# Final sums of a conditioning vector: columns through VectorE and small products, gates through two float32r products

## The chip, the cores and the metric

The kernel runs on one core of a Trainium2 chip. The metric is the device time of one execution in microseconds (us). TensorE (PE, with its weight loads as PEld), VectorE (DVE), ScalarE (ACT) and GpSimd (POOL) each work through their own instructions in the order in which the program placed them; SyncE (SP) issues nearly all loads of weights.

## The reference

Two decoder layers over 256 tokens of width 2048, all float32. Each layer has a mixer and a SwiGLU feed-forward block, and each block is wrapped alike:

```
def ada_modulation(c, w, b):
    mod = jax.nn.silu(c) @ w + b
    return jnp.split(mod[:, None, :], 6, axis=-1)
...
    sh_m, sc_m, gt_m, sh_f, sc_f, gt_f = ada_modulation(c, aw, ab)
    h = rmsnorm(x, m_pre) * (1.0 + sc_m) + sh_m
    x = x + gt_m * rmsnorm(mixer(h), m_post)
    h = rmsnorm(x, f_pre) * (1.0 + sc_f) + sh_f
    x = x + gt_f * rmsnorm(swiglu(h, wg, wu, wd), f_post)
```

The change concerns `ada_modulation` alone: for each layer a vector of 6 x 2048 numbers (the *sections*: shift, scale and gate for the mixer, and again for the feed-forward block) is the product of one vector with a 2048 x 12288 matrix. That matrix is 100 MB per layer, a third of all bytes that the kernel reads.

## The kernel before

**The large products.** Every weight is loaded in float32 as a tile `w` of 128 x 1024 (512 KB, a ring of 6), and split: ACT casts it to float32r (`wh`, L159), DVE subtracts to get the rest (`wl`, L160). Both go into rings of 3. `mm3` (L234 to L236) makes three float32r products of the two halves with the two halves of the activations. Nearly all of PE's time is in these three lines.

**The conditioning.** The generators `ada`, `ada_scale`, `ada_shift` and `ada_gate` are a background stream: `tick`, called from the loops over the large products, lets the stream take a step at a set rate (`AR`), so that the 100 MB of each layer are loaded between the weights, through the same ring of 6 `w` tiles. The first two sections of layer 0 are computed in `start` and are not touched by the change. Ten sections go through the stream, in the order gm0, hf0, sf0, gf0, hm1, sm1, gm1, hf1, sf1, gf1 (g is a gate, h a shift, s a scale; m the mixer, f the feed-forward block; the digit is the layer).

A section is made in two halves of 1024 columns. A tile `acc` of 128 x 1024 is zeroed by POOL (L340), its first row receives the bias by a small DMA (L341), and for 16 tiles of the matrix DVE adds weight times silu(c) to it (L355, 128 x 1024 each). For the section gm0 PE does that instead (L329), and DVE adds its partial sums (L349). There is one buffer for `acc`: the next half's zeroing waits until the last reader of this one is done.

What remains is to sum `acc` over its 128 partitions. Each half is cut into two pieces of 512 columns (`finish`, called with q = 0 to 3), so a half brings a *pair* of calls:

- shifts and scales need the sums as columns, 128 x 4. `to_cols` makes them with four products of a 128 x 128 piece of `acc` as the stationary operand and a single column of ones (L365). DVE then copies the four columns out (L374 or L385). 6 sections x 4 calls = 24 calls.
- gates need the sums in every partition. One product with a stationary 128 x 128 of ones and `acc` as the moving operand of 512 columns does it (L400), and DVE multiplies by the norm's weights (L402). 4 sections x 4 calls = 16 calls. For gm0 the column of ones is replaced by `sel`, which picks 4 of the 128 partitions.

All these products are in float32; the trace shows each as two instructions of PE.

**What sets the order.** The program is written once; a scheduler places the instructions on each engine by its own estimate of when each will be ready. Only the splits have a raised priority. An engine then runs its list strictly in that order: a DVE instruction that has to wait holds up every DVE instruction behind it, the splits among them.

Of the kernel before, what the change touches and what calls it, by code (L numbers as in the profile page):

```python
# [43 lines left out]
class Net:  # L44
# [49 lines left out]
    def consts(s):  # L94
        nc = s.nc

        def mask(name, op, cm, step, base=0):
            t = s.cst.tile([P, P], F32, name=name)
            nc.gpsimd.memset(t, 1.0)
            nc.gpsimd.affine_select(out=t, in_=t, pattern=[[step, P]], compare_op=op, fill=0.0, base=base, channel_multiplier=cm)  # L100
            return t

        s.ident = mask("ident", ALU.is_equal, 1, -1)
        s.uinc = mask("uinc", ALU.is_ge, -1, 1)
        s.ustr = mask("ustr", ALU.is_gt, -1, 1)
        s.lstr = mask("lstr", ALU.is_gt, 1, -1)
        s.ones = s.cst.tile([P, P], F32, name="ones")
        nc.gpsimd.memset(s.ones, 1.0)

        s.sel = s.cst.tile([P, LINE], F32, name="sel")[:, 0:1]  # L110
        nc.vector.tensor_reduce(out=s.sel, in_=s.ident[:, 0::32], axis=AX.X, op=ALU.add)

    def picks(s):
        nc = s.nc
# [216 lines left out]
    def ada(s, layer, sec, finish, pe=False):  # L331
# [5 lines left out]
        for hf in range(2):  # L337
# [18 lines left out]
                    if g < 15:  # L356
                        yield
            for q in range(2):
                finish(2 * hf + q, halves[q], s.sel if pe else s.ones)
            yield  # L360

    def to_cols(s, acc, e):
        ps = s.tp()
        for m in range(4):
            s.nc.tensor.matmul(ps[:, m : m + 1], lhsT=acc[:, m * P : m * P + P], rhs=e[:, 0:1], start=True, stop=True)  # L365
        return ps

    def ada_scale(s, layer, sec, pre, key, pe=False):
        t = s.cst.tile([P, 16], F32, name="S_" + key)

        def finish(q, acc, e):
            ps = s.to_cols(acc, e)
            qs = slice(4 * q, 4 * q + 4)
            s.nc.vector.scalar_tensor_tensor(out=t[:, qs], in0=ps[:, :4], scalar=1.0, in1=s.V[pre][:, qs], op0=ALU.add, op1=ALU.mult)  # L374
            if q == 3:
                s.mod[key] = t
# [3 lines left out]
    def ada_shift(s, layer, sec, key, pe=False):  # L380
        t = s.cst.tile([P, 16], F32, name="H_" + key)

        def finish(q, acc, e):
            ps = s.to_cols(acc, e)
            s.nc.vector.tensor_copy(t[:, 4 * q : 4 * q + 4], ps[:, :4])  # L385
            if q == 3:
                s.mod[key] = t
# [3 lines left out]
    def ada_gate(s, layer, sec, post, key, pe=False):  # L391
        g = []

        def finish(q, acc, e):
# [2 lines left out]
                g.append(s.b(name="gate"))  # L397
                s.pin(nc.gpsimd.dma_start(out=g[-1], in_=s.a[post][q * 512 : q * 512 + 1024].partition_broadcast(P)))
            ps = s.tp()
            nc.tensor.matmul(ps, lhsT=e[:, 0:1].to_broadcast([P, P]), rhs=acc, start=True, stop=True)  # L400
            gs = g[-1][:, (q % 2) * 512 : (q % 2) * 512 + 512]
            nc.vector.tensor_tensor(out=gs, in0=ps, in1=gs, op=ALU.mult)  # L402
            if q == 3:
# [1243 lines left out]
```

## Time and profile before

| | |
|---|---|
| three runs | 2548.6, 2556.36, 2563.09 us (median 2556.36) |
| the profiled execution | 2552.04 us, its span 2550.3 us |
| granted TensorE clock, mean | 0.978 |
| PE busy | 2433.1 us (95%) |
| DVE busy | 1722.2 us (68%) |
| ACT busy | 1106.1 us (43%) |
| column sums, L365 | 192 instructions of PE, 404 to 1652 us |
| gate sums, L400 | 32 instructions of PE, 242 to 2004 us |

A row of a group names the line, engine, operation, tiles, shapes and count, then the busy time in us and the mean duration of one in ns, then the idle time of the engine just before these instructions with what ended it. A row of the timeline begins with the start in us and the duration in us. Durations of PE instructions overlap, since it works pipelined: what an instruction costs there is the distance from one start to the next. A row of the windows has, after the stretch and its length, the busy time of each engine with its instructions, then the granted clock, the share of time in which the DMA engines were busy, and GB/s.

By time, the stages are: the start of layer 0 to about 320 us, its mixer to about 590 us, the first feed-forward block to 1370 us, the mixer of layer 1 to 1800 us, and the second feed-forward block. The calls in question lie at 242 and 317 us (gm0), 404 and 486 (hf0), 541 and 594 (sf0), 717 and 790 (gf0), 857 and 933 (hm1), 1009 and 1085 (sm1), 1158 and 1225 (gm1), 1304 and 1450 (hf1), 1556 and 1650 (sf1), 1739 and 2003 (gf1), each time a pair.

### The profile page before, as it was taken

The numbers are of one execution on the slowest core, as the hardware profiler recorded it, in microseconds if no ns is written. First come the engines' busy times: TensorE is split into PE (matmuls) and PEld (weight loads), VectorE is DVE, ScalarE is ACT, GpSimd is POOL, SyncE is SP. The second block draws the span as 40 slices with busy tenths as digits, with TensorE's granted clock in tenths as the row PEclk, the third lists the DMA queues.
The fourth block names the chain that finished last, engine by engine and source line by source line (L and its number), as shares of the span: only waits on it lengthen the run. The fifth ranks groups of instructions, "written<-read, shape, count | busy, mean of one in ns | idle before, by whom it ended". The sixth has DMA issues, their size and how long they took to land.

```text
span 2550.3 us, 43246 instructions
## 1 busy us (share of the span) xinstructions
PE 2433.1 (95%) x17510; PEld 2141.5 (84%) x17510; DVE 1722.2 (68%) x2268; ACT 1106.1 (43%) x1385; POOL 91.1 (4%) x153
## 2 busy tenths in 40 slices
PE   5999998997999999999998999999999999999998
PEld 2578877876899899989987897787799889988996
DVE  6856786878677766777778676677655544545456
ACT  3354552435344444433435533444544444443443
POOL 1120011000000000000000000000000000000000
PEclk8999998998999999999999999999999999999999
DMA  8877566686798888998886596788467666666664
GB/s 282 322 245 261 176 214 215 204 312 226 244 313 292 305 285 290 309 317 314 289 273 216 155 289 224 242 282 271 164 215 225 197 191 194 195 190 194 195 191 140
DMA packets 299017, 615.70 MB, mean 241 GB/s; under 512 B 24368, under 2 KB 61680, under 8 KB 298816
## 3 DMA queue, kind: packets, MB, share of 16 engines
q1 hardware_dynamic: 294240, 604.32, 71.5%
q0 software_dynamic: 2304, 4.93, 0.6%
q10 hardware_dynamic: 2272, 3.68, 0.4%
q8 instruction: 137, 2.24, 0.3%
q14 instruction: 64, 0.52, 0.1%
HBM read 610.10 MB, written 2.10 MB: 240 GB/s over the span
## 4 chain that ended last, share of the span: by engine, by line
PE 77%; DVE 8%; DMA 8%; ACT 3%; issue 3%; POOL 0%; ACTq 0%; DVEq 0%; SPq 0%
PE mm L236 23%; PE mm L235 23%; PE mm L234 23%; DMA w<-in_ada_w_dram 6%; DVE wl L160 2%; DVE small L355 1%; PE tp L329 1%; PE tp L365 1%; DMA w<-in_w_out_dram 1%; ACT small L462 1%; ACT small L421 1%; PE tp L1049 1%; ACT wh L159 0%; PE tp L400 0%; DMA w<-in_w_in_dram 0%
## 5 line engine op out<-in xcount | busy, mean ns | idle before, releaser
L159 ACT CAST wh<-w 128x1024 fp32r<-128x1024 f32 x722 | 758.0, 1051 | 1095.6 <-PE mm L235 550.6
L160 DVE TENSOR_TENSOR wl<-w,wh 128x1024 fp32r<-128x1024 f32 x722 | 874.1, 1220 | 476.0 <-ACT wh L159 474.9
L236 PE MATMUL mm<-hhi,wl 128*128 128x256 f32 (+1 forms) x3104 | 865.1, 279 | 10.0 <-DVE wl L160 10.0
L234 PE MATMUL mm<-hhi,wh 128*128 128x256 f32 (+1 forms) x3104 | 866.2, 279 | 0.0
L235 PE MATMUL mm<-hlo,wh 128*128 128x256 f32 (+1 forms) x3104 | 863.3, 278 | 0.0
L236 PEld LDWEIGHTS mm<-hhi,wl 128*128 128x128 f32 (+1 forms) x3104 | 582.8, 188 | 15.2 <-DVE wl L160 13.2
L235 PEld LDWEIGHTS mm<-hlo,wh 128*128 128x128 f32 (+1 forms) x3104 | 583.2, 188 | 2.0 <-issue 1.1
L234 PEld LDWEIGHTS mm<-hhi,wh 128*128 128x128 f32 (+1 forms) x3104 | 581.3, 187 | 4.1 <-issue 2.0
L355 DVE SCALAR_TENSOR_TENSOR small<-w,silu_c,small 128x1024 f32<-128x1024 f32 x288 | 369.0, 1281 | 195.8 <-DMA w<-in_ada_w_dram 187.3
L236 PE MATMUL mm<-wh,alo 128*128 128x512 f32 x656 | 258.2, 394 | 0.0
L235 PE MATMUL mm<-wl,ahi 128*128 128x512 f32 x656 | 256.9, 392 | 0.0
L234 PE MATMUL mm<-wh,ahi 128*128 128x512 f32 x656 | 256.2, 391 | 0.0
L234 PE MATMUL mm<-wh,hhi 128*128 128x512 f32 x440 | 177.1, 406 | 8.1 <-DVE hhi L467 4.2
L235 PE MATMUL mm<-wl,hhi 128*128 128x512 f32 x440 | 177.8, 404 | 3.5 <-DVE wl L160 2.2
L236 PE MATMUL mm<-wh,hlo 128*128 128x512 f32 x440 | 175.2, 399 | 0.7 <-DVE hlo L468 0.7
L235 PEld LDWEIGHTS mm<-wl,ahi 128*128 128x128 f32 x656 | 123.1, 188 | 29.1 <-issue 0.5
L234 PEld LDWEIGHTS mm<-wh,ahi 128*128 128x128 f32 x656 | 123.2, 188 | 27.2 <-ACT wh L159 0.5
L236 PEld LDWEIGHTS mm<-wh,alo 128*128 128x128 f32 x656 | 123.3, 188 | 25.1
L234 PEld LDWEIGHTS mm<-wh,hhi 128*128 128x128 f32 x440 | 83.8, 192 | 27.7 <-ACT wh L159 5.5
L236 PEld LDWEIGHTS mm<-wh,hlo 128*128 128x128 f32 x440 | 84.6, 192 | 22.3 <-issue 2.3
L235 PEld LDWEIGHTS mm<-wl,hhi 128*128 128x128 f32 x440 | 84.4, 192 | 22.4 <-DVE wl L160 3.9
L329 PE MATMUL tp<-w,silu_c 128*32 128x512 f32 x384 | 67.0, 645 | 11.6 <-DMA w<-in_ada_w_dram 6.7
(438 smaller groups left out, 2325.5 us busy)
## 6 DMA issues: line engine op xcount, KB each, us to landing
w<-in_ada_w_dram SPq DMA_DIRECT2D x384, 512.0 KB, 5.2
w<-in_ffn_gate_dram SPq DMA_DIRECT2D x176, 512.0 KB, 4.6
w<-in_ffn_up_dram SPq DMA_DIRECT2D x176, 512.0 KB, 4.5
w<-in_ffn_down_dram SPq DMA_DIRECT2D x176, 512.0 KB, 4.5
w<-in_w_in_dram SPq DMA_DIRECT2D x160, 512.0 KB, 5.2
w<-in_w_out_dram SPq DMA_DIRECT2D x64, 512.0 KB, 5.3
w<-in_s_glu_w_dram SPq DMA_DIRECT2D x8, 512.0 KB, 5.0
x<-in_x_dram SPq DMA_DIRECT2D x4, 512.0 KB, 6.4
```

The lines of the kernel that those rows point to most:

```text
L159: s.nc.scalar.copy(hi, x)
L160: s.subs.append(s.nc.vector.tensor_tensor(out=lo, in0=x, in1=hi, op=ALU.subtract).ins)
L234: mm(ps, lhsT=lhs[0], rhs=rhs[0], start=st, stop=False)
L235: mm(ps, lhsT=lhs[0], rhs=rhs[1], start=False, stop=False)
L236: mm(ps, lhsT=lhs[1], rhs=rhs[0], start=False, stop=en)
L329: s.nc.tensor.matmul(ps[32 * j : 32 * j + 32, :], lhsT=lhsT, rhs=w, start=first, stop=last)
L355: nc.vector.scalar_tensor_tensor(out=acc, in0=wv[:, 0], scalar=s.sc[:, g : g + 1], in1=acc, op0=ALU.mult, op1=ALU.add)
L365: s.nc.tensor.matmul(ps[:, m : m + 1], lhsT=acc[:, m * P : m * P + P], rhs=e[:, 0:1], start=True, stop=True)
L421: s.nc.scalar.activation(out=dump[:, : int(x.free_size())], in_=x, func=AF.Square, accum_out=out)
L462: nc.scalar.activation(out=hf[:, js], in_=ps[:, js], func=AF.Identity, scale=S[:, k : k + 1], bias=H[:, k : k + 1])
L1049: nc.tensor.matmul(pp[:, i * 64 : i * 64 + 64], lhsT=s.s5_win[ig][e][:, i * P : i * P + P], rhs=us[:, i * 64 : i * 64 + 64], start=True, s ...
```

## The change

The columns: DVE turns the 512 columns of `acc` in blocks of 32 x 32 (`transpose`), sums each block along its rows (`tensor_reduce`, 128 x 512 to 128 x 16), and four products of 128 x 32 by 128 x 4 with `idc` (four 32 x 32 identities below one another) add the four groups of partitions. Each of the four writes another 32 partitions of the result. The gates: ACT casts the 512 columns to float32r (`hi`), DVE subtracts to get the rest (`lo`), and two float32r products with a stationary column of ones (or `sel`, both now float32r in the tile `ends`) are added in PSUM.

```diff
+        s.ends = s.cst.tile([P, LINE], F32R, name="ends")
         s.sel = s.cst.tile([P, LINE], F32, name="sel")[:, 0:1]
         nc.vector.tensor_reduce(out=s.sel, in_=s.ident[:, 0::32], axis=AX.X, op=ALU.add)
+        nc.vector.tensor_copy(s.ends[:, 0:1], s.ones[:, 0:1])
+        nc.vector.tensor_copy(s.ends[:, 1:2], s.sel)
...
-                finish(2 * hf + q, halves[q], s.sel if pe else s.ones)
+                finish(2 * hf + q, halves[q], s.ends[:, 1 if pe else 0 :][:, :1])
...
-    def to_cols(s, acc, e):
+    def to_cols(s, acc):
+        nc = s.nc
+        turned, part = s.small([P, 512], tag="t", bufs=6), s.small([P, 16], tag="tcs")
+        nc.vector.transpose(out=turned, in_=acc)
+        nc.vector.tensor_reduce(out=part, in_=turned[:].rearrange("p (b r) -> p b r", r=32), axis=AX.X, op=ALU.add)
+        pv = part[:].rearrange("p (m b) -> p b m", b=4)
         ps = s.tp()
-        for m in range(4):
-            s.nc.tensor.matmul(ps[:, m : m + 1], lhsT=acc[:, m * P : m * P + P], rhs=e[:, 0:1], start=True, stop=True)
+        for b in range(4):
+            nc.tensor.matmul(ps[b * 32 : b * 32 + 32, :4], lhsT=s.idc, rhs=pv[:, b], start=True, stop=True)
         return ps
...
-            nc.tensor.matmul(ps, lhsT=e[:, 0:1].to_broadcast([P, P]), rhs=acc, start=True, stop=True)
+            hi, lo = (s.small([P, 512], F32R, tag="t", bufs=6) for _ in range(2))
+            nc.scalar.copy(hi, acc)
+            nc.vector.tensor_tensor(out=lo, in0=acc, in1=hi, op=ALU.subtract)
+            for i, x in enumerate((hi, lo)):
+                nc.tensor.matmul(ps, lhsT=e.to_broadcast([P, P]), rhs=x, start=i == 0, stop=i == 1)
```

The lines of the changed kernel that matter: the turn is L370, the sum of blocks L371, the small products L375, the cast L411, the subtraction L412, the gate products L414. Unchanged lines move down by up to 14 (`mm3` is L237 to L239, the split's subtraction L163, the accumulation L358, the copies of columns L384 and L395).

The scheduler places the new instructions. First, DVE in the feed-forward block of layer 0, at the first pair of hf1. `H_hf` is the tile of finished columns. Before:

```order
L355 SCALAR_TENSOR_TENSOR small<-w,silu_c,small 128x1024 x2
L160 TENSOR_TENSOR wl<-w,wh 128x1024 x2
L355 SCALAR_TENSOR_TENSOR small<-w,silu_c,small 128x1024
L160 TENSOR_TENSOR wl<-w,wh 128x1024 x5
L385 COPY H_hf_105<-tp 128x4 x2
L160 TENSOR_TENSOR wl<-w,wh 128x1024 x2
```

And changed:

```order
L358 SCALAR_TENSOR_TENSOR small<-w,silu_c,small 128x1024
L163 TENSOR_TENSOR wl<-w,wh 128x1024
L370 STREAM_TRANSPOSE small<-small 128x512 x2
L371 TENSOR_REDUCE small<-small 128x16
L163 TENSOR_TENSOR wl<-w,wh 128x1024
L371 TENSOR_REDUCE small<-small 128x16
L163 TENSOR_TENSOR wl<-w,wh 128x1024
L358 SCALAR_TENSOR_TENSOR small<-w,silu_c,small 128x1024
L163 TENSOR_TENSOR wl<-w,wh 128x1024
L358 SCALAR_TENSOR_TENSOR small<-w,silu_c,small 128x1024
L163 TENSOR_TENSOR wl<-w,wh 128x1024
L395 COPY H_hf_108<-tp 128x4 x2
```

Both turns stand one split behind the last accumulation, and a further split stands between the two sums of blocks.

Second, PE at the same place (the operands `hhi`, `hlo` are the halves of the activations). Before:

```order
L235 MATMUL mm<-hlo,wh 128x256
L236 MATMUL mm<-hhi,wl 128x256
L365 MATMUL tp<-ones,small 128x1 x8
L234 MATMUL mm<-hhi,wh 128x256
L235 MATMUL mm<-hlo,wh 128x256
```

And changed:

```order
L238 MATMUL mm<-hlo,wh 128x256
L239 MATMUL mm<-hhi,wl 128x256
L375 MATMUL tp<-small,idc 32x4 x8
L237 MATMUL mm<-hhi,wh 128x256
L238 MATMUL mm<-hlo,wh 128x256
```

The eight small products stand between the same two large ones as the eight products with a column did; so it is at all pairs from 717 us on.

Third, DVE at the end of layer 0's mixer, at the last pair of sf0 (`S_sf` its columns, `x` the residual, L138, L139, L141 and L142 steps of a reciprocal root). Before:

```order
L139 SCALAR_TENSOR_TENSOR small<-small 128x1
L160 TENSOR_TENSOR wl<-w,wh 128x1024
L138 TENSOR_SCALAR small<-small 128x1
L374 SCALAR_TENSOR_TENSOR S_sf_102<-tp,vcols 128x4
L139 SCALAR_TENSOR_TENSOR small<-small 128x1
L374 SCALAR_TENSOR_TENSOR S_sf_102<-tp,vcols 128x4
L138 TENSOR_SCALAR small<-small 128x1
L160 TENSOR_TENSOR wl<-w,wh 128x1024
L139 SCALAR_TENSOR_TENSOR small<-small 128x1
L527 SCALAR_TENSOR_TENSOR x<-y,small,x 128x512 x4
```

And changed:

```order
L142 SCALAR_TENSOR_TENSOR small<-small 128x1
L163 TENSOR_TENSOR wl<-w,wh 128x1024
L141 TENSOR_SCALAR small<-small 128x1
L370 STREAM_TRANSPOSE small<-small 128x512
L142 SCALAR_TENSOR_TENSOR small<-small 128x1
L370 STREAM_TRANSPOSE small<-small 128x512
L141 TENSOR_SCALAR small<-small 128x1
L371 TENSOR_REDUCE small<-small 128x16
L142 SCALAR_TENSOR_TENSOR small<-small 128x1
L371 TENSOR_REDUCE small<-small 128x16
L541 SCALAR_TENSOR_TENSOR x<-y,small,x 128x512 x4
L384 SCALAR_TENSOR_TENSOR S_sf_105<-tp,vcols 128x4 x2
```

The copies of the columns, which wait for PE, have moved from ahead of the update of `x` to behind it, and the second split (L160) behind them; four new instructions stand in their place. The order of SP's loads is unchanged throughout.

More of the change, by code (lines that the diff above doesn't have):

```diff
@@ L371, in finish @@
         def finish(q, acc, e):
-            ps = s.to_cols(acc, e)
+            ps = s.to_cols(acc)
             qs = slice(4 * q, 4 * q + 4)
@@ L383, in finish @@
         def finish(q, acc, e):
-            ps = s.to_cols(acc, e)
+            ps = s.to_cols(acc)
             s.nc.vector.tensor_copy(t[:, 4 * q : 4 * q + 4], ps[:, :4])
```

## The prediction

> **What bounds the kernel now.** I read the page first, then the busy times by stage, then who waited for whom.
>
> ```profile
> span 2550.3 us, 43246 instructions
> PE 2433.1 (95%) x17510; PEld 2141.5 (84%) x17510; DVE 1722.2 (68%) x2268; ACT 1106.1 (43%) x1385; POOL 91.1 (4%) x153
> PE 77%; DVE 8%; DMA 8%; ACT 3%; issue 3%; POOL 0%; ACTq 0%; DVEq 0%; SPq 0%
> 500.00:600.00 100.00, 84.71 (x351) 66.89 (x349) 81.83 (x117) 37.33 (x51) 2.87 (x4) 0.90 0.90 316
> 700.00:1300.00 600.00, 593.02 (x4322) 554.95 (x4322) 437.06 (x391) 242.73 (x244) 13.21 (x19) 1.00 0.87 300
> ```
>
> The reader is to see that PE is the bound, and not everywhere alike. From 700 to 1300 us it is busy 593 of 600 us, at the full clock, while VectorE has 163 us idle. From 500 to 600 us it is busy 85 of 100 and the DMA engines 90%: there a microsecond saved on PE buys less, and one added to VectorE, which releases the tiles that the loads go into, may cost.
>
> What VectorE waits for, and what PE waits for, between 700 and 1300 us and (second row) 700 and 1370 us:
>
> ```profile
> DVE small L355 <- DMA w<-in_ada_w_dram: 94.2, 63, 3.3
> PE mm L236 <- DVE wl L160: 7.0, 10, 1.8
> ```
>
> VectorE's accumulation often stands waiting for its tile, with the splits queued behind it, and ten times that came through to PE: 7 us. So added work on VectorE has a way to PE, a narrow one.
>
> **The columns: what PE saves.** One pair of calls in the trace, 16 instructions between two large products:
>
> ```profile
> 1304.30 0.28 PE L236 MATMUL mm<-hhi,wl 128*128 128x256 f32 x1
> 1304.42 1.84 PE L365 MATMUL tp<-ones,small 128*128 128x1 f32 x16
> ...
> 1306.33 0.28 PE L235 MATMUL mm<-hlo,wh 128*128 128x256 f32 x1
> ```
>
> From the pair's start to the second large product behind it are 1.91 us; one large product of 256 columns takes 0.12, so the pair costs 1.80, some 0.11 for each instruction though each moves one column: what it pays is the stationary 128 x 128.
>
> The new pair has 16 instructions too, but with 32 stationary columns. The trace has that shape in two places: 256 instructions with 16 or 48 moving columns, and a block of 16 with 512. For the floor there is a third, 32 x 32 pieces that work side by side:
>
> ```profile
> 0.00:2550.00 2550.00, 10.79 (x256) 10.09 (x256) 0.98 0.73 241
> 197.92 0.28 PE L236 MATMUL mm<-hhi,wl 128*128 128x256 f32 x1
> 198.12 1.92 PE L329 MATMUL tp<-w,silu_c 128*32 128x512 f32 x16
> 199.98 0.38 PE L234 MATMUL mm<-hhi,wh 128*128 128x256 f32 x1
> 200.20 0.28 PE L235 MATMUL mm<-hlo,wh 128*128 128x256 f32 x1
> 406.06 1.53 PE L1307 MATMUL tp<-small,T 32*32 32x16 f32 x128
> 407.52 0.80 PE L234 MATMUL mm<-wh,hhi 128*128 128x512 f32 x1
> ```
>
> The first row is L998 alone: 10.79 us for 256, 0.042 each. The block at 198 us shows what entering and leaving the narrow shape costs: 0.20 from the last large product instead of 0.11 or 0.12 (0.09 more), 0.22 instead of 0.11 behind it (0.11 more), and 1.86 for work that at 0.43 a round (the rate of the gate products below) fills four rounds of 1.72 (0.14 more); 0.34 in all. With 16 x 0.042 a new pair costs 1.01. The floor is 16 x 0.011 (128 in 1.46 us) and 0.34: 0.52. The ceiling is 1.80, no gain. I take 0.95, nearest to the row with the same stationary shape, since 4 columns are fewer than 16: a gain of **0.85 for a pair** (0 to 1.28).
>
> A page gives a lower price for this step: by the Trainium skill (TensorE: Matmul & The Clock Gate, section LDWEIGHTS) a weight load takes its columns divided by 1.2 ns, whatever the rows, 27 ns for 32 columns; by that a pair would cost 0.77, an estimate from the page, and the whole sum would come out 1.8 us lower. The 0.11 for 128 columns agrees with it.
>
> Eight pairs from 857 us on: -6.8 us. Of the four earlier ones, two (404 and 541 us) have PE at work up to the call and behind it: -1.7. The others are below.
>
> **The gates: what PE saves.** A pair of calls before, and the pace of a float32r product of 512 columns:
>
> ```profile
> 717.37 1.88 PE L400 MATMUL tp<-small,ones 128*128 128x512 f32 x4
> ...
> 719.20 0.28 PE L235 MATMUL mm<-hlo,wh 128*128 128x256 f32 x1
> 857.11 0.39 PE L235 MATMUL mm<-wl,ahi 128*128 128x512 f32 x1
> 857.34 0.39 PE L236 MATMUL mm<-wh,alo 128*128 128x512 f32 x1
> ```
>
> Four instructions cost 1.83 less the 0.11 of one large product, 1.72, or 0.43 each. The four new products go at 0.23: 0.92. **0.80 saved for a pair.** Six pairs from 717 us on and the first of gm0: -5.6. ACT's new casts (618 ns, below) are 16 in all, on an engine with over half its time free.
>
> **What VectorE is given.** The nearest rows are the same forms elsewhere:
>
> ```profile
> L1310 DVE STREAM_TRANSPOSE T<-T 128x512 f32<-128x512 f32 x4 | 2.8, 706 | 0.0
> L1417 DVE TENSOR_REDUCE small<-small 128x4 f32<-128x512 f32 x4 | 2.7, 677 | 1.1 <-ACT small L1413 1.1
> L160 DVE TENSOR_TENSOR hlo<-xT,hhi 128x512 fp32r<-128x512 f32 x8 | 5.3, 686 | 0.2
> L159 ACT CAST hhi<-xT 128x512 fp32r<-128x512 f32 x8 | 4.8, 618 | 8.4 <-DVE xT L1482 8.4
> ```
>
> A pair of column calls adds 2 x 706 + 2 x 677 = 2.77 us, a pair of gates 2 x 686 = 1.37. That is 12 x 2.77 + 8 x 1.37 = 44 us in all, 30.4 of it in the fourteen pairs from 717 us on. The new wait is PE's: L375 stands in PE's list where L365 stood, and everything on PE stands behind it. What covers it is the time between the last accumulation and PE's turn, with VectorE's busy time in it as third number:
>
> ```profile
> 708.12:717.37 9.25, 9.25 (x82) 9.11 (x82) 8.28 (x9) 4.11 (x4) 0.00 (x0) 1.00 0.91 307
> 850.46:857.57 7.11, 7.11 (x32) 5.82 (x31) 4.72 (x5) 2.23 (x3) 0.00 (x0) 1.00 0.94 334
> 1075.66:1085.07 9.41, 9.06 (x55) 7.86 (x54) 8.29 (x9) 4.10 (x4) 0.00 (x0) 1.00 0.92 313
> 1219.92:1225.42 5.50, 5.50 (x50) 5.50 (x50) 4.63 (x5) 2.11 (x2) 0.00 (x0) 1.00 0.90 303
> 1294.88:1304.42 9.54, 8.59 (x73) 8.40 (x72) 5.86 (x6) 3.09 (x3) 0.00 (x0) 1.00 0.85 287
> 1639.42:1650.20 10.78, 10.78 (x52) 8.94 (x52) 8.26 (x10) 4.89 (x6) 0.00 (x0) 1.00 0.80 259
> 466.79:485.95 19.16, 16.86 (x107) 14.44 (x107) 16.24 (x49) 9.32 (x14) 0.00 (x0) 1.00 0.58 191
> ```
>
> At 1304 us 3.68 of 9.54 are idle, more than the 2.77. Five late pairs are short: by 0.40, 0.38, 1.65, 0.50 and 0.25 in the order of the rows, 3.2 together. The rings hold up to two split tiles ahead, so I let half reach PE: **+1.5** (0 to all 30.4). Without that cover every microsecond added to VectorE is one that the splits, and PE with them, come later.
>
> **The three early pairs.** At 486 us VectorE is busy 16.24 of 19.16 us and each piece of it is waited for: 2.77 added, 0.85 saved, **+1.9** (-0.85 to +2.77). The second pair of gm0 (317 us) saves 0.80 on PE, but in the changed order its four products are strung out between others, each needing a cast or a subtraction first: +0.3 (-0.8 to +1.3). The last pair of sf0 lies in the norm between mixer and feed-forward:
>
> ```profile
> 596.37 0.16 DVE L374 SCALAR_TENSOR_TENSOR S_sf<-tp,vcols 128x4 f32<-128x4 f32 x1 [0.57 <-PE tp L365]
> 598.07 0.16 DVE L374 SCALAR_TENSOR_TENSOR S_sf<-tp,vcols 128x4 f32<-128x4 f32 x1 [1.48 <-PE tp L365]
> 598.33 1.22 DVE L160 TENSOR_TENSOR wl<-w,wh 128x1024 fp32r<-128x1024 f32 x1
> 606.38 6.27 PE L458 MATMUL tp<-small,x 128*128 128x128 f32 x32 [8.35 <-issue]
> ```
>
> PE idles 8.35 us there whatever it saves; VectorE's list is the path. It gains 2.77, and loses the two waits (2.05), since the copies move behind the update of x, and 1.22 until the split's new place: that split then holds up the root behind it. I take 0 (-0.5 to +0.7).
>
> **The sum**: -6.8 - 1.7 - 5.6 + 1.5 + 1.9 + 0.3 + 0 = -10.4 us. The profiled execution took 2552.04, so 2541.6; the median of the runs stands 4.3 above that, and from it I predict **2546 us**, 0.4% less.
>
> **Rivals.** (1) *The small products work side by side and all of VectorE's work is covered.* The four write four separate groups of 32 partitions, as those of L1307 do; against it, L998's 0.042 is all that a 128-row shape of few columns shows. At the floor of 0.52 ten pairs save 12.8; with the gates' 5.6 and the three early pairs at their low ends (-0.85 - 0.8 - 0.5) and nothing through VectorE: -20.5, 2536 us.
>
> (2) *The columns bring nothing*: each small product, going to another group of columns of the array, waits for the one before, and costs the 0.11 of the old. For it speaks that the block at 198 us pays 0.34 around its products; against it, L998 pays 0.042 with a load for each product. The sum is then -5.6 + 1.5 + 2.8 + 0.3 = -1.0: 2555 us. The Trainium skill speaks for a weaker form of it (TensorEngine Tiling (Array Packing), sections Key Properties and Instruction Overhead): a change of tiling mode drains the array, and a product of one moving column lasts as long as one of sixty, so that tiling gains nothing from a dimension that is small already. By the first, the price is paid twice a pair, as the 0.34 has it; by the second, all the gain must come from the narrower stationary side.
>
> (3) *Slower: the splits come late.* VectorE works in order, so each turn and block sum delays the next split, that releases its `w` tile later, the next load starts later, and the accumulation behind it waits, with the next split in its queue: the way by which 7 us came to PE already. Against it: 163 us idle in 600, and the slack above. With a share f of the 30.4 us reaching PE the sum is -11.9 + 30.4 f; it turns slower at f = 0.39, and at 0.8 it is +12.4, 2569 us.
>
> **How the numbers follow.** The forecast has 0.56, rival (1) 0.20, (2) 0.12, (3) 0.12. About what a measurement can tell from no change is 0.5%, 12.8 us. Rival (1) is faster by more; of the forecast's share some 0.20 lies beyond 12.8 too, since 10.4 is close to it and its terms are good to 4 us: faster 0.40. Of (3) a little over half is beyond it on the other side: slower 0.07. The rest, 0.53, is the same. The range leaves out the low end of (1) and the upper half of (3): 2534 to 2560.
>
> **What would show it.** A pair of L375 spanning 0.8 to 1.1 us between large products (0.5: rival 1; 1.8: rival 2). Four L414 in 0.92. No PE idle time before L375 or L414 from 717 us on; if there is some, released by L371 or L412, my cover failed. PE's wait for the splits from 700 to 1370 us near 8.5 instead of 7.0; at 15 or more, rival (3). The stretch from 455 to 600 us longer by 0 to 2 us. A gain over 20 us, or any loss, would make the prediction wrong.

## The result, and the profile after

The changed kernel takes 2635.29 us (median of 4 runs, 2629.4 to 2638.4) against 2558.06 for the kernel before on the same chip: a ratio of 1.030, 95% interval 1.0272 to 1.0327. It is 77 us slower, where 10 us less were predicted. The profiled execution took 2637.96 us, 86 more than the one of before, and its page begins:

```profile
span 2636.2 us, 43284 instructions
PE 2468.3 (94%) x17510; PEld 2151.7 (82%) x17510; DVE 1755.9 (67%) x2334; ACT 1111.2 (42%) x1401; POOL 90.5 (3%) x153
PE 46%; DMA 21%; DVE 12%; issue 5%; ACT 2%; POOL 0%; DVEq 0%; ACTq 0%; POOLq 0%
```

PE's share of the chain that ends last has fallen from 77% to 46%, and the transfers have taken its place. The busy times of the two stretches that the prediction compared show where:

```profile
500.00:600.00 100.00, 82.31 (x349) 62.87 (x347) 85.71 (x124) 39.49 (x53) 1.43 (x2) 0.93 0.89 310
700.00:1300.00 600.00, 561.23 (x3911) 512.90 (x3911) 413.63 (x383) 225.76 (x232) 13.21 (x19) 0.99 0.83 275
```

From 700 to 1300 us PE has 39 us idle instead of 7, and the loads run at 275 GB/s instead of 300. Who waits there (the first row is from 700 to 1300 us, the others from 700 to 1370):

```profile
DVE small L358 <- DMA w<-in_ada_w_dram: 167.0, 88, 4.0
PE mm L239 <- DVE wl L163: 26.5, 25, 2.6
PE mm L238 <- DVE wl L163: 15.8, 15, 2.4
```

VectorE's accumulations wait 167 us for their tiles instead of 94, and 42.3 us of that come through to PE as waits for splits, where 7.0 stood before and 8.5 were predicted.

The sums themselves are cheaper than predicted. PE's timeline around one pair of column calls and one pair of gate calls:

```profile
1041.85 0.28 PE L239 MATMUL mm<-hhi,wl 128*128 128x256 f32 x1
1042.06 0.31 PE L375 MATMUL tp<-small,idc 128*32 128x4 f32 x16
1042.29 0.38 PE L237 MATMUL mm<-hhi,wh 128*128 128x256 f32 x1
1042.52 0.28 PE L238 MATMUL mm<-hlo,wh 128*128 128x256 f32 x1
...
724.86 0.28 PE L239 MATMUL mm<-hhi,wl 128*128 128x256 f32 x1
724.97 1.10 PE L414 MATMUL tp<-small,ends 128*128 128x512 f32 x4
725.90 0.28 PE L237 MATMUL mm<-hhi,wh 128*128 128x256 f32 x1
```

From 1041.85 to 1042.52 are 0.67 us; without the two large products in it (0.12 each) the pair of columns costs 0.43 instead of 1.80. The gates cost 0.93 instead of 1.72. With ten pairs of columns and seven of gates beside working PE that is 10 x 1.37 + 7 x 0.79 = 19.2 us saved, if all go like these two. (Nine of the ten and all seven do, within 0.03; the pair at 404 us has two other products between its own.) VectorE's new instructions last what the nearest rows said, 42.8 us in all:

```profile
L370 DVE STREAM_TRANSPOSE small<-small 128x512 f32<-128x512 f32 x24 | 16.3, 695 | 0.1
L371 DVE TENSOR_REDUCE small<-small 128x16 f32<-128x512 f32 x24 | 15.8, 671 | 0.0
L412 DVE TENSOR_TENSOR small<-small 128x512 fp32r<-128x512 f32 x16 | 10.7, 683 | 0.0
```

So every price held or was better, and the kernel lost 86 us in the trace. To see where, the distance from the start of each PE product to the next was sorted into three. A large product has a **pace**: what its distance exceeds 113.4 ns (256 columns) or 229 ns (512) by, up to 25 ns. More than 25 ns counts as a **pause** of PE. The **rest** is what stands behind all other products, waits that follow them included. The large products at 113.4 and 229 ns make 2088.8 us in every run, and with 9 us ahead of the first product and 10 or 11 behind the last the parts make up each span. In us:

| run | span | pace | pause | of it, splits 150 to 375 | rest |
|---|---|---|---|---|---|
| before | 2550.3 | 12.2 | 112.0 | 19.9 | 317.8 |
| changed | 2636.2 | 54.1 | 175.4 | 74.7 | 298.3 |
| difference | +85.9 | +41.9 | +63.4 | +54.8 | -19.5 |

(Splits 150 to 375, of 762, are the feed-forward block of layer 0, 745 to 1396 us before.) There are two losses, not one. PE pauses 63 us more, 55 of them in this block. And all large products run at a slower pace, which costs 42 us and is no wait at all. A window in the second feed-forward block, where PE works without a pause at the full clock on products of 256 columns alone, shows the pace. Before:

```profile
2150.00:2250.00 100.00, 100.00 (x885) 100.00 (x884) 50.04 (x43) 42.81 (x43) 0.00 (x0) 1.00 0.62 195
```

And in the changed kernel:

```profile
2180.00:2280.00 100.00, 100.00 (x851) 100.00 (x851) 48.18 (x42) 40.86 (x42) 0.00 (x0) 1.00 0.60 187
```

885 products in 100 us are 113.0 ns each, 851 are 117.5; the two or three that reach over the ends of a window are counted with them.

### The profile page after: what moved, and what is told of

It reads as the page before. It is cut to its first block, busy times and chain, and to the rows that moved or that the text cites. A ratio compares the mean times of both kernels' runs of the same rounds, so it can differ in the third digit from the quotient of the medians.

```text
span 2636.2 us, 43284 instructions
## 1 busy us (share of the span) xinstructions
PE 2468.3 (94%) x17510; PEld 2151.7 (82%) x17510; DVE 1755.9 (67%) x2334; ACT 1111.2 (42%) x1401; POOL 90.5 (3%) x153
## 4 chain that ended last, share of the span: by engine, by line
PE 46%; DMA 21%; DVE 12%; issue 5%; ACT 2%; POOL 0%; DVEq 0%; ACTq 0%; POOLq 0%
DMA w<-in_ada_w_dram 19%; PE mm L237 14%; PE mm L239 14%; PE mm L238 14%; DVE small L358 5%; DVE wl L163 4%; DMA w<-in_w_out_dram 1%; ACT small L476 1%; DMA small<-in_ada_b_dram 1%; ACT small L435 1%; DMA w<-in_ffn_down_dram 0%; ACT wh L162 0%; DVE small L141 0%; DVE y L530 0%; DVE small L370 0%
## 5 line engine op out<-in xcount | busy, mean ns | idle before, releaser
L163 DVE TENSOR_TENSOR wl<-w,wh 128x1024 fp32r<-128x1024 f32 x722 | 871.9, 1218 | 428.7 <-ACT wh L162 423.8
L239 PE MATMUL mm<-hhi,wl 128*128 128x256 f32 (+1 forms) x3104 | 874.7, 282 | 29.9 <-DVE wl L163 29.3
L237 PE MATMUL mm<-hhi,wh 128*128 128x256 f32 (+1 forms) x3104 | 873.9, 282 | 2.3 <-DVE qt L669 2.1
L239 PEld LDWEIGHTS mm<-hhi,wl 128*128 128x128 f32 (+1 forms) x3104 | 584.0, 188 | 38.7 <-DVE wl L163 37.0
L237 PEld LDWEIGHTS mm<-hhi,wh 128*128 128x128 f32 (+1 forms) x3104 | 583.8, 188 | 6.2 <-ACT e L650 2.2
L358 DVE SCALAR_TENSOR_TENSOR small<-w,silu_c,small 128x1024 f32<-128x1024 f32 x288 | 369.5, 1283 | 322.7 <-DMA w<-in_ada_w_dram 299.6
L237 PE MATMUL mm<-wh,ahi 128*128 128x512 f32 x656 | 259.5, 396 | 0.0
L239 PE MATMUL mm<-wh,alo 128*128 128x512 f32 x656 | 259.4, 395 | 0.0
L237 PE MATMUL mm<-wh,hhi 128*128 128x512 f32 x440 | 177.9, 408 | 9.1 <-ACT wh L162 5.8
L239 PE MATMUL mm<-wh,hlo 128*128 128x512 f32 x440 | 176.9, 403 | 0.2 <-DVE hlo L482 0.2
L237 PEld LDWEIGHTS mm<-wh,ahi 128*128 128x128 f32 x656 | 123.3, 188 | 30.0
L239 PEld LDWEIGHTS mm<-wh,alo 128*128 128x128 f32 x656 | 123.4, 188 | 29.1
L237 PEld LDWEIGHTS mm<-wh,hhi 128*128 128x128 f32 x440 | 83.7, 192 | 30.7 <-ACT wh L162 7.2
L239 PEld LDWEIGHTS mm<-wh,hlo 128*128 128x128 f32 x440 | 84.3, 192 | 20.9 <-DVE hlo L482 0.8
L332 PE MATMUL tp<-w,silu_c 128*32 128x512 f32 x384 | 67.3, 633 | 10.1 <-ACT silu_c L326 5.9
```

The lines of the kernel that those rows point to most:

```text
L163: s.subs.append(s.nc.vector.tensor_tensor(out=lo, in0=x, in1=hi, op=ALU.subtract).ins)
L237: mm(ps, lhsT=lhs[0], rhs=rhs[0], start=st, stop=False)
L239: mm(ps, lhsT=lhs[1], rhs=rhs[0], start=False, stop=en)
L332: s.nc.tensor.matmul(ps[32 * j : 32 * j + 32, :], lhsT=lhsT, rhs=w, start=first, stop=last)
L358: nc.vector.scalar_tensor_tensor(out=acc, in0=wv[:, 0], scalar=s.sc[:, g : g + 1], in1=acc, op0=ALU.mult, op1=ALU.add)
```

## The experiments

All ratios are against the kernel before, on the same chip, with 95% intervals.

| run | edit | median us | ratio |
|---|---|---|---|
| hold | changed, acc released at PE's turn | 2592.1 | 1.0124 [1.0091, 1.0158] |
| load | before, VectorE's column work added, unused | 2587.3 | 1.0119 [1.0082, 1.0155] |
| early | before, acc released early by a copy | 2602.2 | 1.0176 [1.0139, 1.0214] |
| pin | changed, accumulations behind the splits | 2580.6 | 1.0080 [1.0050, 1.0109] |
| padsm | before, 128 unused bytes among the small tiles | 2585.5 | 1.0105 [1.0079, 1.0131] |
| padcst | before, 128 unused bytes among the constants | 2562.7 | 1.0017 [1.0003, 1.0031] |
| layhold | hold, operands at the addresses of before | 2568.9 | 1.0040 [1.0027, 1.0054] |
| laypin | pin, operands at the addresses of before | 2548.6 | 0.9952 [0.9937, 0.9967] |
| lay | changed, operands at the addresses of before | 2619.9 | 1.0244 [1.0224, 1.0264] |
| pinb | before, accumulations behind the splits | 2543.9 | 0.9946 [0.9929, 0.9964] |
| lp64 | laypin, 64 unused bytes | 2579.4 | 1.0084 [1.0062, 1.0106] |
| lp192 | laypin, 192 unused bytes | 2591.3 | 1.0138 [1.0109, 1.0167] |
| laygates | gates alone, addresses of before | 2584.7 | 1.0113 [1.0084, 1.0143] |
| laycols | columns alone, addresses of before | 2574.6 | 1.0070 [1.0049, 1.0090] |
| lp256 | laypin, 256 unused bytes | 2542.8 | 0.9943 [0.9922, 0.9964] |

### What the change moved: the release of acc

POOL zeroes `acc` for the next half as soon as its last reader is done. The waits of that zeroing between 700 and 1430 us name the reader. Before:

```profile
POOL small L340 <- PE tp L365: 365.3, 5, 77.2
POOL small L340 <- PE tp L400: 315.9, 4, 109.8
```

Changed:

```profile
POOL small L343 <- DVE small L370: 393.5, 5, 80.6
POOL small L343 <- DVE small L412: 333.7, 4, 102.6
```

Before, PE released the tile, at its place in PE's list 5 to 11 us behind the last accumulation in the late windows that the prediction shows. Now VectorE's turn or subtraction does, a few instructions behind it. Between 700 and 1300 us the traces have POOL's zeroing start 7.4 to 11.5 us behind the last accumulation before, and 2.4 to 7.1 us behind it changed. The next half's accumulations can be placed that much earlier, and the scheduler places them so. The loads stay in their order on SyncE. How far an accumulation stands ahead of its load can be counted in the lists: splits whose loads come ahead of its load, less splits that stand ahead of it on VectorE. The mean over the 16 accumulations of each half, from the second half of gf0 to gm1 (these are the 112 accumulations of which the expectations speak):

```
             gf0   hm1        sm1        gm1
before       1.1   0.4  1.6   1.1  1.4   0.7  0.7
changed      1.8   2.4  2.9   2.9  2.9   2.6  2.3
hold         1.1   0.4  1.6   1.1  1.4   0.7  0.7
early        1.9   2.6  2.8   2.9  2.9   2.7  2.7
pin         -0.3  -0.3 -0.1   0    0    -0.1 -0.3
laygates     1.8   2.4  1.6   1.1  1.4   0.7  1.9
laycols      1.1   0.4  2.3   2.9  2.9   2.6  0.7
```

At 2.9, nearly three splits whose tiles are loaded earlier stand behind an accumulation that waits for a later load. This made theory A; theory B was the prediction's rival (3), VectorE's added work; theory C new waits between PE and VectorE at the sums.

**hold**: PE reads `acc` once more behind the products, so that it is released at PE's turn again.

```diff
             nc.tensor.matmul(ps[b * 32 : b * 32 + 32, :4], lhsT=s.idc, rhs=pv[:, b], start=True, stop=True)
+        nc.tensor.matmul(ps[:32, 8:9], lhsT=s.idc, rhs=acc[:, 0:1], start=True, stop=True)
...
                 nc.tensor.matmul(ps, lhsT=e.to_broadcast([P, P]), rhs=x, start=i == 0, stop=i == 1)
+            nc.tensor.matmul(s.tp()[:32, 0:1], lhsT=s.idc, rhs=acc[:, 0:1], start=True, stop=True)
```

> The changed kernel, and behind each call's products PE reads one column of acc in one more small product, so that acc is again released at PE's turn. All of VectorE's added work stays (44 us). In the list of VectorE the accumulations then stand as in the kernel before: over the 112 accumulations of hm1 to gm1 each stands on average 1.0 splits ahead of the place that its load has among the loads (before 1.0, changed 2.6). Theory A (the accumulations moved ahead of splits, and wait there for their tiles): nearly the whole loss comes back, to what the prediction had plus 40 small products of 2 instructions at 0.05 to 0.11 us, so 2546 + 4 to 9, ratio 0.995 to 1.003; VectorE's wait for the tiles of the accumulations near 190 us instead of 300. Theory B (VectorE's added work delays the splits): no change from the changed kernel, 2635 us, ratio 1.03. Theory C (the new waits between PE and VectorE at the sums): no change either, 2635.

**load**: the kernel before, with the turns and block sums made for nobody.

```diff
+        turned, part = s.small([P, 512], tag="t", bufs=6), s.small([P, 16], tag="tcs")
+        s.nc.vector.transpose(out=turned, in_=acc)
+        s.nc.vector.tensor_reduce(out=part, in_=turned[:].rearrange("p (b r) -> p b r", r=32), axis=AX.X, op=ALU.add)
         ps = s.tp()
         for m in range(4):
             s.nc.tensor.matmul(ps[:, m : m + 1], lhsT=acc[:, m * P : m * P + P], rhs=e[:, 0:1], start=True, stop=True)
```

> The kernel before, and in each column call VectorE turns acc and sums its blocks too, with nobody reading the result; the products are the old ones and PE releases acc. Adds 24 x 1.38 = 33 us to VectorE and nothing to PE; the accumulations keep their places (1.0 splits ahead on average, as before). Theory A: 2556 to 2564 us, ratio 1.000 to 1.003. Theory B: three quarters of the loss, about +58, 2615 us, ratio 1.023. Theory C: no change, 2557.

**early**: the kernel before, with a copy that releases `acc`.

```diff
             for q in range(2):
-                finish(2 * hf + q, halves[q], s.sel if pe else s.ones)
+                c = s.small([P, 512], tag="t", bufs=6)
+                nc.scalar.copy(c, halves[q])
+                finish(2 * hf + q, c, s.sel if pe else s.ones)
```

> The kernel before, and ScalarE copies each 512 columns of acc into another tile from which the old float32 products read, so that acc is released by ScalarE, early. VectorE gets no work; ScalarE gets 40 copies of 0.62 us. The accumulations of hm1 to gm1 then stand 2.7 splits ahead of their loads on average (before 1.0, changed 2.6). Theory A: the loss is there without the change's sums, and about the 10 us more that those save on PE: 60 to 90 us, ratio 1.023 to 1.035; VectorE's wait for the tiles of the accumulations near 300 us. Theory B: no change, 2557 (ScalarE has over half its time free). Theory C: no change, or a few us for PE's wait for the copy.

**pin**: the changed kernel, with each accumulation ordered behind the last split written before it (`s.subs` holds the splits' subtractions).

```diff
-                    nc.vector.scalar_tensor_tensor(out=acc, in0=wv[:, 0], scalar=s.sc[:, g : g + 1], in1=acc, op0=ALU.mult, op1=ALU.add)
+                    with s.tc.issue_after(s.subs[-1]):
+                        nc.vector.scalar_tensor_tensor(out=acc, in0=wv[:, 0], scalar=s.sc[:, g : g + 1], in1=acc, op0=ALU.mult, op1=ALU.add)
```

> The changed kernel, and each accumulation may not be placed ahead of the last split that the program wrote before it, so that VectorE takes the tiles in the order in which they are loaded: 0.1 splits behind its load's place on average, none ahead. All sums as in the changed kernel. Theory A: the loss comes back, and of the waits that the kernel before has (187 us of VectorE, 14 us of PE for splits) a part as well: 2530 to 2548, ratio 0.990 to 0.997. If the accumulations now come too late and hold their tiles longer, 2550 to 2570. Theory B and C: 2635, ratio 1.03.

Measured: 2592, 2587, 2602, 2581. None is where one theory alone puts it; pin is 33 us above theory A's range. hold brings back 43 of 77 us, not all. early loses 43 with no work on VectorE and no change of the sums, so the order costs by itself, but not everything. And load costs 28 us, which theory A had at 0 to 8 and theory B at 58. The waits of the accumulations from 700 to 1400 us sort the runs by the order. In the changed kernel:

```profile
DVE small L358 <- DMA w<-in_ada_w_dram: 194.2, 102, 4.0
```

In hold:

```profile
DVE small L358 <- DMA w<-in_ada_w_dram: 89.5, 63, 3.0
```

In early:

```profile
DVE small L355 <- DMA w<-in_ada_w_dram: 199.5, 114, 3.9
```

PE's pauses between splits 150 and 375 do the same: 74.7 us changed, 70.1 early, 17.9 hold, 17.9 load, 19.9 before. With VectorE's column work in it, load has no more pauses there than before, and hold, with all of the added work, has none more either: **theory B is refuted for this block**. Theory C goes with it, since hold has all the sums. What load, hold and pin have in common with the changed kernel, and early has not, is the pace: 54.9, 53.7, 55.5 and 54.1 us, against 12.6 in early and 12.2 before. (Of the single products of 256 columns without a pause, by the traces 31% are slow in before and early, not the 20 to 22% that the expectations give, and 93 to 97% in the other four.)

How the order costs, step by step, stands in the chain of waits of the changed kernel at 980 to 1010 us (start, duration, what):

```profile
979.70 1.30 DVE small L358
981.00 0.02 issue
981.01 4.18 DMA w<-in_ada_w_dram
...
985.29 1.29 DVE small L358
986.58 0.02 issue
986.60 4.82 DMA w<-in_ada_w_dram
...
991.51 1.29 DVE small L358
```

An accumulation ends, its end releases the load for the next one, which takes 4 to 5 us, and the next accumulation stands at the head of VectorE's list until it lands. Between these waits VectorE's timeline has two splits each time. From 979.70 to 1004.65 us there are four such rounds (one of them with two accumulations), 24.95 us with eight splits, 6.24 for two; PE uses two up in 48 products, 5.65 at 117.8 ns. So PE starves by a tenth; over splits 150 to 375 its pauses are 74.7 of 709 us. In hold the same 30 us are a chain of large products alone. Over 800 to 1300 us the shares of the chain by line are, in the changed kernel:

```profile
by line: DMA w<-in_ada_w_dram 55.0%; DVE small L358 11.7%; DVE wl L163 8.4%; issue 8.0%; PE mm L239 4.3%; PE mm L238 4.0%; PE mm L237 3.8%; DMA small<-in_ada_b_dram 1.6%; DVE sg L580 0.9%; DVE small L370 0.7%; POOL small L343 0.6%; DVE y L5
```

In hold:

```profile
by line: PE mm L239 30.1%; PE mm L237 30.1%; PE mm L238 29.7%; DMA w<-in_ada_w_dram 5.1%; DVE wl L163 1.5%; DVE small L358 1.1%; issue 0.9%; PE tp L415 0.7%; DVE alo L588 0.2%; PE tp L375 0.2%; ACT wh L162 0.2%; PE tp L416 0.2%; DVE small L
```

### What the change moved besides: the addresses

In all four kernels of the slow pace there is one more small tile, `tcs` (2 x 64 bytes in each partition). The pools lie one behind the other in SBUF, the memory on the chip: constants, the ring of weights, small tiles, `blk` with the activations. Before, `blk` starts 291.75 x 256 bytes behind the ring by the compiled program's layout, noted ahead of the run lp64 (the traces hold no addresses); with `tcs` it starts 128 bytes further off. (In the changed kernel `ends` moves both by another 64.)

**padsm** and **padcst**: the kernel before, with nothing but unused bytes.

```diff
+        for _ in range(2):
+            s.nc.gpsimd.memset(s.small([P, 16], tag="pad"), 0.0)
```
```diff
+        s.nc.gpsimd.memset(s.cst.tile([P, 32], F32, name="pad"), 0.0)
```

> The kernel before, and two unused tiles of 64 bytes in the pool of small tiles, zeroed once at the start; nothing else. They move the pool blk, in which the activations of the large products lie, by 128 bytes against the ring of weights, as the changed kernel's new tile tcs does. In the four runs so far the large products of 256 columns come either each 113.4 or each 117.8 ns, the pace being chosen at each pause of PE: before and early 20 to 22% of them at the slow pace, changed, hold, load and pin 96% or more. Theory D (where the operands lie in SBUF sets the pace): nearly all products slow, 8700 x 4.4 ns = 38 us more at most, about +28 as with load: 2587 us, ratio 1.011. If the pace comes from the added work instead: no change, 2558.

> The kernel before, and one unused tile of 128 bytes in the pool of constants, so that the ring of weights, the small tiles and blk all move by 128 bytes together. If the distance between weights and activations sets the pace: no change, 2558 us and 20% of the products slow. If the place of blk by itself does: as with the pad among the small tiles, 2587 us.

Measured: padsm 2585.5, as expected, with 55.2 us of pace. 128 bytes that nobody reads cost 27 us. padcst, which moves weights and activations together, costs 4, with 18.5 us of pace. The window of the second feed-forward block in padsm:

```profile
2150.00:2250.00 100.00, 100.00 (x851) 100.00 (x850) 47.76 (x41) 41.52 (x42) 0.00 (x0) 1.00 0.63 186
```

In padcst:

```profile
2150.00:2250.00 100.00, 100.00 (x885) 100.00 (x884) 49.96 (x43) 44.08 (x45) 0.00 (x0) 1.00 0.66 193
```

So it is the distance between the operands, and their common place counts for little. This also explains load: its 28 us and 54.9 us of pace are those of padsm, so they are the tile `tcs`, not the work.

**layhold**, **laypin** and **lay** put `ends` and `tcs` where tiles of other stages lie, so that the ring and `blk` are where they were (`sel` moves to the slot of an old small tile).

```diff
-        s.sel = s.cst.tile([P, LINE], F32, name="sel")[:, 0:1]
+        s.sel = s.small([P, 1], tag="gr", bufs=1)
...
-        turned, part = s.small([P, 512], tag="t", bufs=6), s.small([P, 16], tag="tcs")
+        turned, part = s.small([P, 512], tag="t", bufs=6), s.small([P, 16, 1], tag="s5er")[:, :, 0]
```

> The run hold (changed kernel, acc released at PE's turn), with the new tiles ends and tcs put where other tiles are no longer or not yet in use, so that the ring of weights and blk lie exactly as before. Theories A and D together: the order of the accumulations and the pace are as before, and the prediction's sum is left, -10 us, plus 4 to 9 for the 40 held reads: 2548 to 2556 us, ratio 0.996 to 0.999, and 20% of the products slow. If VectorE's added work costs by itself (theory B): 2592 as hold.

> The run pin (changed kernel, each accumulation behind the last split written before it), laid out as before in the same way. Theories A and D: 2580 less the 30 to 38 us of the pace, 2543 to 2551, ratio 0.994 to 0.997, faster than both kernels. Otherwise 2580.

> The changed kernel with ends and tcs put where other tiles are no longer or not yet in use, so that the ring of weights and blk lie as before; the accumulations stand as in the changed kernel (2.5 splits ahead of their loads over hm1 to gm1). With hold and layhold it gives the fourth corner: order moved or not, operands moved or not. Moved operands cost 23 us between layhold and hold and 27 in padsm; the moved order cost 43 between hold and the changed kernel. If the two add up: 2635 less 23 to 32, 2603 to 2612 us, ratio 1.018 to 1.022. If the late order costs only because the products are slow as well: 2575 or less.

Measured: 2568.9, 2548.6, 2619.9. laypin came out as expected and beats both kernels. layhold is 13 us above the expected range, lay 8. The four corners:

| | operands as before | operands moved | cost of moving |
|---|---|---|---|
| order as before | layhold 2568.9 | hold 2592.1 | 23 |
| order moved | lay 2619.9 | changed 2635.3 | 15 |
| cost of the order | 51 | 43 | |

Each costs with or without the other, and they add up but for 8 us. The cost of the order is a little low: the held reads make a late pair of gates 0.70 us longer and a pair of columns 0.11 us, some 7 us in all, which only the runs with the order as before carry.

layhold takes 10.5 us more than before; its trace is 15.7 longer, by 14.1 of pace, 12.4 of pauses (0.9 of them in the block above) and -10.3 of rest. Most of that pace, 11.9 us, comes behind split 550, in the second feed-forward block. There the place of the operands is not the reason, since it is that of before. Two runs told of below, both at the addresses of before, show what differs. With the new gates alone (laygates):

```profile
2150.00:2250.00 100.00, 100.00 (x851) 100.00 (x850) 48.59 (x42) 40.75 (x41) 0.00 (x0) 1.00 0.64 189
```

With the new columns alone (laycols):

```profile
2150.00:2250.00 100.00, 100.00 (x885) 100.00 (x884) 52.20 (x46) 43.65 (x44) 0.00 (x0) 1.00 0.66 195
```

The last pair of gf1, the last of all calls, stands ahead of this stretch. In the five kernels at a distance of 291.75 or 292.75 x 256 bytes with new gates (layhold, laypin, lay, laygates, lp256) PE goes from the fast pace to the slow one across that pair, and splits 550 to the end have 11.5 us of pace each time. In the five with the old float32 gates (before, early, padcst, pinb, laycols) it is at the fast pace behind the pair, in padcst after the slow one ahead of it. So the new gate calls at this place bring a slow pace that lasts to the end, a cost of the change that no price covered; which property of theirs does it was not tried. Taking the 7 and the 11.9 us off what layhold loses leaves a gain of 3 to 8 us (by its trace, by its medians), an estimate.

### What remains of the change, and the better kernels

**pinb**: the kernel before with the order of pin, by the same edit.

> The kernel before with the accumulations behind the last split written before each, and nothing else. What differs from laypin is the change itself, with order and layout alike. The change's sums are worth 13.9 us of PE by the prediction's prices (10 pairs of columns at 0.85, 7 of gates at 0.80, less 0.2 for the early ones), less what VectorE's 44 us cost. If those cost nothing with this order: laypin (2548.6) plus 10 to 14, 2559 to 2563, ratio 1.000 to 1.002, and the whole gain of laypin over before is the change's own. If the order alone brings the gain: 2545 to 2550, ratio 0.995.

Measured 2543.9, ratio 0.9946 [0.9929, 0.9964], as if the order alone brought the gain: laypin, which has the change's sums on top, is not faster. The traces say what cancels: laypin against pinb has -20.7 us of rest and +11.1 of pauses, and +14.9 of pace. Ahead of split 100 (the start and mixer of layer 0) the pauses are 10.1 longer and the rest 9.3 shorter, and split 100 starts within 0.6 us of the same time: there the two cancel, and no time is lost. So the order is worth 14.6 us to the kernel before, and the sums would be worth about 10 (20.7 less 11.1, an estimate) at an equal pace. The pace is not equal, and 11.9 us of the difference are those behind the new gates. In the medians the sums gain nothing at this order. Nor is the order of pinb good everywhere: in the traces it is 14.8 us behind before at split 100 and 8.5 ahead at the end.

**lp64**, **lp192**, **lp256**: laypin with a pad of 16, 48 or 64 floats.

```diff
+        s.nc.gpsimd.memset(s.small([P, 16], tag="pad", bufs=1), 0.0)
```

> laypin with one unused tile of 64 bytes among the small tiles: blk starts 291.75 + 0.25 = 292 times 256 bytes behind the ring of weights instead of 291.75 times (before) or 292.25 times (changed). If the distance sets the share of slow products, a third share shows here: 2530 to 2580 us; no direction is expected, since nothing so far shows which distances are good. If only the shift by 128 is bad, 2545 to 2552.

> laypin with one unused tile of 192 bytes among the small tiles: blk 292.5 times 256 bytes behind the ring of weights. As lp64: by the distance a share of slow products of its own, 2530 to 2580 us; otherwise 2545 to 2552.

> laypin with one unused tile of 256 bytes among the small tiles: blk 292.75 times 256 bytes behind the ring of weights, the same quarter as before (291.75). If the pace goes by the distance within 256 bytes: as laypin, 2543 to 2555 us, and paces of 113.4 and 117.8 ns both to be seen. If it goes by something wider: any of the times seen with other pads, 2575 to 2595.

Measured: 2579.4, 2591.3 (11 us above its range) and 2542.8, with 53.0, 65.4 and 17.5 us of pace (laypin 23.3). The window from 2150 to 2250 us in lp64:

```profile
2150.00:2250.00 100.00, 100.00 (x835) 100.00 (x835) 46.98 (x42) 40.75 (x41) 0.00 (x0) 1.00 0.63 182
```

In lp192:

```profile
2150.00:2250.00 100.00, 100.00 (x845) 100.00 (x844) 50.03 (x44) 41.79 (x42) 0.00 (x0) 1.00 0.64 185
```

119.8 and 118.3 ns for a product. Of the four distances modulo 256 bytes that were tried, each at one layout, the one of before is the best, and 256 bytes more give it again. lp256 and pinb are the fastest versions found, 0.9943 and 0.9946, and not told apart.

**laygates** and **laycols**: one half of the change alone, addresses as before.

> The kernel before with the new gates alone (old float32 columns), operands laid out as before. The accumulations behind gates move ahead (over hm1 to gm1 1.55 splits ahead on average; before 1.0, both halves of the change 2.54), those behind columns stay. The order costs 51 us between layhold and lay; by the shift of the places gates have 0.55 of 1.54, 18 us. With 5.6 us saved on PE and up to 12 for a slower pace: 2568 to 2582 us, ratio 1.004 to 1.009. If VectorE's part is what costs and not the order, 11 us of added work at most: 2553 to 2569.

> The kernel before with the new columns alone (old float32 gates), operands laid out as before. The accumulations behind columns move ahead (1.84 splits on average). By the shift of the places columns have 0.84 of 1.54 of the order's 51 us, 28 us, less 8.5 saved on PE, up to 12 for a slower pace and some for 33 us of VectorE's work: 2576 to 2595 us, ratio 1.007 to 1.014; more than laygates.

Measured 2584.7 and 2574.6, so laygates is slower than laycols, against the expectation. In PE's pauses between splits 150 and 375 the halves do stand as the shift of the accumulations has it: 19.9 before, 37.8 laygates, 55.2 laycols, 84.8 lay. In time the other terms turn it round: laygates has 21.9 of pace, 11.5 of it behind its last pair of gates, and no gain in the rest (318.4); laycols has 5.5 and 296.9. Each half loses only where it moves the accumulations: from split 175 to 200, behind gf0, laygates falls back 6.8 us and laycols 0.5; from 225 to 250, among the columns, laygates gains 0.4 and laycols falls back 14.8.

## Why the prediction was wrong

**The columns, -0.85 a pair**: right in sign, too small. 1.37 was measured, better than the floor of the 32 x 32 pieces (0.43 against 0.52 for a pair). The four small products go at 14 ns each, near the 11 of the pieces that work side by side, as rival (1) had it; its 2536 us fell with the order. **The gates, -0.80**: right, 0.79. **VectorE's durations**: right to 2%.

**VectorE's work leaks +1.5**: right where it was put. In the feed-forward block pauses are 19.9 before, 17.9 with the column work alone (load), 17.9 in hold, 20.8 in layhold; the cover was there. The **three early pairs** (+2.2 in sum) are not told apart from the other early calls: all that the change does ahead of split 100 comes to -0.6 us between pinb and laypin. With 20.7 less 11.1 the change would be worth 9.6 us on equal order and pace, an estimate. The predicted 10.4 is near it by luck in part: the columns save 5 us more than priced, and as much is lost again in places that were not traced one by one.

**The step that failed** is the silent one under the sum: that everything not named stays as it was. Two things above all did not, the order and the addresses; a third, the pace behind the last new gates, is 11.5 us where the addresses are as before. First, the order. The prediction looked at where the turn stands and what covers it. It did not ask what the turn releases: `acc`, in the feed-forward block up to 9 us earlier than PE did. The piece of VectorE's list on record shows it, two accumulations (L358) between the turns and the copies, where before five splits and the copies came first. Nothing moved on SyncE or, in these places, on PE, and that was taken for the whole. This term, put at nothing, is 43 to 51 us.

Second, the addresses. A new tile of 128 bytes was costed at nothing since nobody waits for it. It is 15 to 27 us, in a term that the profile shows as no wait and no idle time.

**Rival (3)** has its symptoms: waits for splits of 42 us, far over the 15 it named. Its cause, the added work, does not: load has the work and no more pauses there, early has the pauses and no work. The last link of its chain, an accumulation at the head of the list with the splits behind it, was described rightly. Its trigger was the place of the accumulations, not 30 us of work. **Rival (2)** fell with the 0.43.

**PE before L375**: from 717 us on no idle time was predicted, and none was measured. In the whole run it is 6.3 us, all of it ahead of 700 us:

```profile
PE tp L375 <- DVE small L371: 6.3, 3, 5.6
```

What stays open: why PE lands at one pace or the other, and why the new gates settle it where they do. It was not tried whether reads collide; the runs show only that the distance of the operands shifts the odds and the paces.

## What to carry to other kernels

When an instruction is moved to another engine, ask which buffer its operand frees, when, and what a scheduler will place there instead: the last reader of a buffer sets the order of the next user's work. Compare the whole list of the in-order engine with the order of the loads, not only the neighbourhood of the change; an instruction that waits for a later load than those behind it holds up everything. And when a tile is added, look whether the large operands still lie at the same distance; if all instructions of a kind take some ns more, pad before looking for a wait.

## What was not expected of the hardware

PE's large products have two paces, and which one holds is settled at a pause. In the kernel before, around a wait for a split:

```profile
922.90 0.28 PE L234 MATMUL mm<-hhi,wh 128*128 128x256 f32 x1
923.01 0.28 PE L235 MATMUL mm<-hlo,wh 128*128 128x256 f32 x1
925.04 0.39 PE L236 MATMUL mm<-hhi,wl 128*128 128x256 f32 x1 [1.75 <-DVE wl L160]
925.26 0.28 PE L234 MATMUL mm<-hhi,wh 128*128 128x256 f32 x1
925.38 0.28 PE L235 MATMUL mm<-hlo,wh 128*128 128x256 f32 x1
925.50 0.28 PE L236 MATMUL mm<-hhi,wl 128*128 128x256 f32 x1
```

Ahead of it the products follow at 0.113 us, behind it at 0.118, and so on until 999 us. Products of 512 columns show nearly the same (229 and 233.3), so between these two paces it is a price for a product, not for a column. With both operands 291.75 x 256 bytes apart, 113.4 and 117.8 ns both occur; at 292.25 nearly all products of 256 columns take 117.8, at 292 nearly all take 120, at 292.5 most take 118.5 or 120. The longer form does not follow: at 292 a product of 512 columns takes 227 ns, less than the 229 of before. The Trainium skill (TensorE: Matmul & The Clock Gate, section Step-by-step: what each phase is for) says that PE has two independent read ports and that loading the next weights does not take bandwidth from the running product. No run here shows the ports by themselves. If the Trainium skill is right in this, something else ties the two operands: an unused pad that moves only the one operand against the other changed the time by 27 us.

Small products that write four separate groups of 32 partitions take 0.23 us for 16 of them (1042.06 to 1042.29 above), 14 ns each, where the same stationary width in one group took 42 ns each with 16 or 48 moving columns (L998). The held reads, of that width too, with one moving column and all to one group, add 0.10 to 0.11 us to a pair for four, 25 to 28 ns each.
